# All 22 side blocks projected in one pass per token part, and TensorE's and VectorE's order fixed in both scans

## The chip, the cores and the metric

The kernel runs on one core of a Trainium2 chip. The metric is the device time of one execution in microseconds (us). The kernel before took 2149.41 us, the median of 3 runs (2149.09 to 2152.09).

## What is computed

One layer over 2048 latent tokens and 256 context tokens of 1024 channels: normalise and modulate, one wide projection, three groups of mixers (centred pooling, a bidirectional RWKV-7 scan, a bidirectional HGRN2 scan), each with a SiLU gate, then one output projection with a residual and a norm. The context only gives the scans their first state.

```python
p_lat = (_layer_norm(h_x) * (1.0 + sc_l[:, None]) + sh_l[:, None]) @ w_in[l]
p_ctx = (_layer_norm(h_ctx) * (1.0 + sc_c) + sh_c) @ w_in[l]
pv_l, u_l, fh_l, g_l = _split_proj(p_lat)
...
y_rc, y_rl = _rwkv_branch(u_c, u_l, ...)
o_hc, o_hl = _hgrn_branch(fh_c, fh_l, ...)
pool_l = _pool_branch(pv_l, True, pool_w[l], pool_scale[l])
mix_l = jnp.concatenate([pool_l, y_rl, o_hl], axis=-1) * jax.nn.silu(g_l)
new_x = _layer_norm(ALPHA * h_x + gt_l[:, None] * (mix_l @ w_out[l])) * ln_g[l] + ln_b[l]

# one step of the RWKV scan (per head, per token)
S = (S * w_t[:, :, None, :] - sa[..., None] * (kk_t * a_t)[:, :, None, :]
     + v_t[..., None] * k_t[:, :, None, :])
# one chunk of the HGRN scan
o = inter + jnp.einsum('bhts,bhsv->bhtv', scores, i_c)
S = (jnp.exp(g_last[:, :, 0, :])[..., None] * S
     + jnp.einsum('bhsk,bhsv->bhkv', k_c * jnp.exp(g_last - g), i_c))
```

## The kernel before

The program has four stages, one after the other.

**Front** (to about 508 us). It normalises x, keeps the normalised x in DRAM (`s_x`), projects the channels that RWKV needs, and forms RWKV's chunk operands.

**RWKV scan.** 36 chunks of 64 tokens (4 of context, 32 latent) are scanned in both directions at once, one `step` (L847) per chunk. On TensorE (PE) a step has `py` (state times kr), mask products into the same tile, `pu`, and `zp` (L883; its tile is also named `pu`). VectorE (DVE) adds the old state (`tz`, L887) and multiplies by the decay (`zbd`, L889), which the next step's `py` reads. ScalarE copies `pp` and `uv` in between. Work ahead of a step: `start` (L703) loads a chunk's operands, forms the products `pa` and masks them on DVE into `at`; `gather` (L754) writes 32x32 blocks to DRAM (`sd`); every 4 chunks `solve` (L768) loads 96 such systems as `m` and solves them by substitution in 31 pairs of DVE instructions (L779 a product into `tm`, L782 a subtraction from `o`), and writes `so`; `merge` (L806) loads from `so` (tile `nn`), transposes it on DVE, and completes the inverse with small PE products. `solve` runs LEAD (7) chunks ahead of the step that needs it. The loop at L942 has one iteration per chunk, and calls pieces of these generators (`go`) in an order written by hand. Inside `manual_schedule` that order is PE's; the other engines' order is chosen by the scheduler, which takes instructions as it thinks them ready.

**The filler** (L529). Beside the scan, PE projects the 22 blocks of 128 channels that RWKV doesn't need (HGRN's q, z of both directions and i; pooling; the gates). The unit between two yields is 6 of the 24 matmuls of a block on up to 512 tokens: three groups of 8 (high by high, low by high, high by low half of a split fp32). `split` makes the halves of x: a cast on ScalarE (`fxh`) and a difference on DVE (`fxl`). GpSimd splits the weights (`fwl`). `Beside` (L635) paces it: each call adds a number to what is due and runs whole units; after a BORDER, where a token part begins, it holds for HOLD calls. 18 blocks over three token parts run in the RWKV scan (R_FIL: from iteration -6, 9.4 units in each, the rest at the scan's end). Two pool blocks and two gate blocks follow in HGRN over three parts of their own, for which x is loaded and split once more.

**HGRN scan.** A window of 256 context or latent tokens (9 windows, each direction) has `hlevels` (L1004): loads, ScalarE activations, the diagonal scores (`pd`, L1055: 6 matmuls of 128x128 by 2 columns, then one DVE product into `sc`, L1056), and levels in which PE forms scores, DVE copies them under a mask (L1046), multiplies `qp` (L1069) and `tot` (L1072), GpSimd `ks`. `hsteps` (L1077) transposes `ks` into `kt`, and walks the window's 4 chunks: PE's `po` and `ps`, DVE's state `sbd` (L1116). `out_weights` (L1121) loads w_out in eight slices through one buffer `fwf`, scales each by the gate on GpSimd (L1128), casts on ScalarE (`fxh`, `woh`; L219), and takes the difference on DVE (`fxl`, `wol`; L220). The pieces of all these are given due times (`at`, L652), sorted and emitted (`follow`, L657); the scheduler then sets each engine's order.

**Output.** Pooling, readouts, gates, the output projection and the last norm, from about 1911 us on.

## Time and profile before

| | |
|---|---|
| median of 3 runs | 2149.41 us (2149.09 to 2152.09) |
| the profiled execution's own time | 2153.85 us |
| its span | 2151.8 us |
| mean granted clock of TensorE | 0.903 |
| PE busy | 1877.4 us (87%), 18306 instructions |
| PE weight load busy | 1593.8 us (74%) |
| DVE busy | 1470.2 us (68%), 3045 |
| ScalarE (ACT) busy | 954.1 us (44%), 1809 |
| GpSimd (POOL) busy | 808.4 us (38%), 729 |

The span runs from the first to the last record of the profiled execution; its own time is 2.05 us longer. The shares are means over four stages that differ, so they don't say what bounds any one of them. Weight load overlaps PE's matmuls. The clock is what the throttle granted TensorE, as a share of full speed.

### The profile page before, as it was taken

To read this page: it belongs to the slowest core of one execution; us is meant where nothing else is said; L and a number is where in the kernel's file an instruction comes from. 1 tells how busy PE (TensorE), PEld (TensorE's weight loads), DVE (VectorE), ACT (ScalarE), POOL (GpSimd) and SP (SyncE) were. 2 spreads that over 40 slices of the span, in tenths; PEclk is the share of its full clock that TensorE was granted. 3 is DMA by queue.
4 is the path that set the end of the run, shared out by engine and by line. 5 is a ranking of instruction groups with operands and counts; after the bars stand their busy time and mean duration, and the time that the engine had idled before them with its cause. 6 is when DMAs were issued, how large, how long until landed. Compare 5 with 4: busy or idle time off the path is not lost. (4 is left out here: it accounts for less than half of the span.)

```text
span 2151.8 us, 46723 instructions
## 1 busy us (share of the span) xinstructions
PE 1877.4 (87%) x18306; PEld 1593.8 (74%) x18306; DVE 1470.2 (68%) x3045; ACT 954.1 (44%) x1809; POOL 808.4 (38%) x729
## 2 busy tenths in 40 slices
PE   4788899994989979999979999968989998878996
PEld 1677788893777768877868788757877776657896
DVE  2788899886546646475473762189788788879862
ACT  3876786663123333333333233455444645322321
POOL 0144355545211322322323323454334435624653
PEclk7899999996999989999979999968888997589998
DMA  6544444328655565655666444442322323545531
GB/s 247 195 136 144 142 131 126 106 74 252 187 147 150 171 184 164 182 143 164 174 180 192 139 129 136 152 132 82 109 81 70 124 80 115 176 150 187 194 128 59
DMA packets 290915, 313.68 MB, mean 146 GB/s; under 512 B 85572, under 2 KB 246468, under 8 KB 289672
## 3 DMA queue, kind: packets, MB, share of 16 engines
q1 hardware_dynamic: 280680, 280.29, 43.3%
q10 hardware_dynamic: 4896, 17.83, 2.5%
q0 software_dynamic: 5120, 12.59, 1.8%
q8 instruction: 144, 2.36, 0.5%
q14 instruction: 75, 0.61, 0.1%
HBM read 213.88 MB, written 96.74 MB: 144 GB/s over the span
## 5 line engine op out<-in xcount | busy, mean ns | idle before, releaser
L220 POOL TENSOR_TENSOR fwl<-fwf,fwh 128x1024 fp32r<-128x1024 f32 x66 | 158.7, 2405 | 422.3 <-ACT fwh L219 369.3
L565 PE MATMUL fps<-fxh,fwh 128*128 128x512 f32 (+1 forms) x952 | 230.7, 375 | 31.0 <-ACT fxh L219 28.4
L565 PE MATMUL fps<-fxl,fwh 128*128 128x512 f32 (+1 forms) x952 | 217.2, 362 | 0.0
L565 PE MATMUL fps<-fxh,fwl 128*128 128x512 f32 (+1 forms) x952 | 211.6, 357 | 0.0
L565 PEld LDWEIGHTS fps<-fxh,fwh 128*128 128x128 f32 x952 | 160.4, 201 | 63.4 <-ACT fxh L219 34.7
L565 PEld LDWEIGHTS fps<-fxl,fwh 128*128 128x128 f32 x952 | 160.2, 199 | 24.1 <-issue 1.0
L565 PEld LDWEIGHTS fps<-fxh,fwl 128*128 128x128 f32 x952 | 158.7, 196 | 23.8
L779 DVE TENSOR_TENSOR tm<-m,o 96x31 f32<-96x31 f32 (+15 forms) x279 | 117.4, 421 | 60.3 <-DMA m<-sd 52.2
L904 POOL TENSOR_TENSOR ys<-ys,pp 64x384 f32<-64x384 f32 x64 | 76.6, 1196 | 198.7 <-ACT ys L901 191.6
L336 PE MATMUL ps<-xh,wh 128*128 128x258 f32 x768 | 125.4, 304 | 17.5 <-ACT wh L219 11.9
L1116 DVE SCALAR_TENSOR_TENSOR sbd<-sbd,tot,ps 64x64 f32<-64x64 f32 x432 | 120.5, 279 | 25.7 <-PE ps L1111 16.7
L1044 PE MATMUL pl<-qb,ks 128*64 128x64 f32 x2304 | 108.4, 252 | 30.3 <-DVE sc L1046 22.9
L1039 ACT COPY qb<-qp 64x384 f32<-64x384 f32 x192 | 99.6, 519 | 77.7 <-DVE qp L1069 33.8
L724 DVE TENSOR_TENSOR at<-pa,cst 128x384 f32<-128x384 f32 x144 | 74.1, 548 | 81.9 <-PE pa L722 81.8
L336 PEld LDWEIGHTS ps<-xh,wh 128*128 128x128 f32 x768 | 106.0, 198 | 30.6 <-ACT wh L219 13.3
L1044 PEld LDWEIGHTS pl<-qb,ks 128*64 128x64 f32 x2304 | 94.1, 161 | 45.5 <-issue 29.3
L782 DVE TENSOR_TENSOR o<-o,tm 96x31 f32<-96x31 f32 (+15 forms) x279 | 115.8, 415 | 8.3
L336 PE MATMUL ps<-xh,wl 128*128 128x258 f32 x768 | 118.6, 294 | 0.0
L1069 POOL TENSOR_TENSOR ks<-ks,tot 128x384 f32<-128x384 f32 x90 | 90.5, 1014 | 74.6 <-PE pl L1044 72.7
L336 PE MATMUL ps<-xl,wh 128*128 128x258 f32 x768 | 116.0, 289 | 0.0
L336 PEld LDWEIGHTS ps<-xh,wl 128*128 128x128 f32 x768 | 104.6, 196 | 5.7 <-issue 5.2
L336 PEld LDWEIGHTS ps<-xl,wh 128*128 128x128 f32 x768 | 102.3, 192 | 4.9 <-issue 4.6
(230 smaller groups left out, 4449.0 us busy)
## 6 DMA issues: line engine op xcount, KB each, us to landing
fwf<-in_w_in_dram SPq DMA_DIRECT2D x66, 512.0 KB, 4.2
xt<-in_x_dram ACTq DMA_DIRECT2D x32, 512.0 KB, 4.9
s_kr<-kr SPq DMA_DIRECT2D x54, 256.0 KB, 2.3
s_bk<-bk SPq DMA_DIRECT2D x54, 256.0 KB, 2.5
bks<-s_bk SPq DMA_DIRECT2D x72, 192.0 KB, 3.2
krs<-s_kr SPq DMA_DIRECT2D x72, 192.0 KB, 3.5
bk<-s_bk SPq DMA_DIRECT2D x72, 192.0 KB, 3.0
kr<-s_kr SPq DMA_DIRECT2D x72, 192.0 KB, 3.1
```

The source lines that it names most:

```text
L220: eng.tensor_tensor(out=wl, in0=wf, in1=wh.bitcast(F32), op=ALU.subtract)
L336: PE.matmul(ps[:, 0:TG + 2], a[:, k, :], b[:, k, :], start=(i == 0), stop=(i == 23))
L565: PE.matmul(ps[:, 0:n], a[:, k, :], b[k][:, o:o + n], start=(i == 0), stop=(i == 23))
L724: V.tensor_tensor(out=at[:, h], in0=pa[h], in1=cst[:, C_MASK[d]].unsqueeze(1).broadcast_to([P, NPR, P]), op=ALU.mult)
L779: V.tensor_tensor(out=tv, in0=m[:, j:j + 1, j + 1:32].broadcast_to([nrow, na, nb]), in1=o[:, 0:na, j:j + 1].broadcast_to([nrow, na, nb]), ...
L782: V.tensor_tensor(out=o[:, 0:na, j + 1:32], in0=o[:, 0:na, j + 1:32], in1=tv, op=ALU.subtract)
L904: G.tensor_tensor(out=ys[vr], in0=ys[vr], in1=pp[d][vr], op=ALU.add)
L1039: S.copy(out=qb[hh, :, :, h, :].rearrange("q p c (i b) -> q (p c) i b", b=b), in_=src[hh].rearrange("q p (c i j b) -> q (p c) i j b", c=nc ...
L1044: PE.matmul(pl[64 * (c % 2):64 * (c % 2) + 64, :, p, c // 2, :], ks[:, p, CH * c:CH * c + CH], qb[:, p, c, :, :], start=True, stop=True)
L1069: eng.tensor_tensor(out=v_, in0=v_, in1=tv[:, :, :, 1 - par:2 - par].broadcast_to([P, NPR, nb, b]), op=ALU.mult)
L1116: V.scalar_tensor_tensor(out=sn[hh, p, hh], in0=so_[hh, p, hh], scalar=tot[hh, p, c:c + 1], in1=ps[hh, p, :], op0=ALU.mult, op1=ALU.add)
```

## The change

**The filler** takes all 22 blocks in each of the three token parts (context and tokens 0 to 511; 1280 to 2047; 512 to 1279), so x is loaded and split once. The loads of x are issued two slices ahead, across parts too. The split of a part's 8 slices is spread over four BORDER yields, two slices each; HOLD is gone, and a call to the pacer ends at a BORDER. 20 units run ahead of the RWKV loop and 7.6 in each of its 43 iterations; what is left goes to HGRN, 2.2, 1.9 or 1.0 units a slot.

**Order.** `manual_schedule` now covers PE and DVE, in the RWKV loop and in HGRN: DVE's instructions, too, stand in program order. In the RWKV loop `solve` has a yield behind its load of `m`, and the load is issued at the end of the iteration that gathers its last chunk; `merge` issues its loads one yield ahead of the transposes. In HGRN the due times are replaced by 14 slots per window: each runs one piece of a level (`l0`, `l1`) and of the steps of the window before (`s0`, `s1`, `k0`, `k1`), and some filler. In the iteration before the last the rest of the filler runs in the first slot and a slice of w_out after each slot.

**The diagonal** changes its form: per direction and window it takes 12 matmuls instead of 6, each of 64 rows of q by 64 columns of `hsl`, with 128 columns moving, and two DVE products of half the size. **`kt`** is copied by ScalarE in two pieces, not three.

```diff
-R_FIL = (-6, 9.4)
+R_FIL = (20, 7.6)
+H_FIL = (2.2, 1.9, 1.0)
...
     def filler(parts, blocks):
-        for part in parts:
+        def load(part, k):
+            xs = fp.tile([P, FTOK], F32, name="fxs", bufs=2)
+            o = 0
+            for t0, n in part:
+                QX.dma_start(out=xs[:, o:o + n], in_=s_x[:, k, t0:t0 + n])
+                o += n
+            return xs
+        xs = [load(parts[0], k) for k in range(2)]
+        for pi, part in enumerate(parts):
...
-                split(xs[:, 0:n_all], xh[k][:, 0:n_all], xl[k][:, 0:n_all], V)
+                split(xs[k % 2][:, 0:n_all], xh[k][:, 0:n_all], xl[k][:, 0:n_all], V)
+                if k + 2 < KB:
+                    xs[k % 2] = load(part, k + 2)
+                elif pi + 1 < len(parts):
+                    xs[k % 2] = load(parts[pi + 1], k % 2)
+                if k % 2:
+                    yield BORDER
...
             G.memset(o.rearrange("q a t -> q (a t)")[:, 0:32 * 32:33], -1.0)
+            yield 1
             for j in range(31):
...
                 ws[n][d]["uv"] = uv
+            yield 1
             ab = [(sub(0, 0), sub(0, 1)), (sub(1, 1), sub(1, 0))]
...
-        with tc.manual_schedule(engines={mybir.EngineType.PE}):
+        with tc.manual_schedule(engines={mybir.EngineType.PE, mybir.EngineType.DVE}):
+            for _ in range(KB // 2):
+                pace(0)
+                next(fill)
+            run(fill, R_FIL[0])
             for n in range(-LEAD, NCH):
...
                 go("late", n + 1, late)
+                go("mer", n + 1, merge)
                 solving(7)
...
                 go("stp", n, step, None)
+                if s_ % SB == SB - 1:
+                    go("sol", s_ // SB, solve)
                 beside(n, 0.22)
             for k, g in gen.items():
                 run(g)
-            run(fill1)
...
-                pd = psl.tile([P, 2, NPR, nm], F32, name="pl")
-                for m in range(nm):
+                pd = [psl.tile([P, NPR, nm, CH], F32, name="pl") for _ in range(2)]
+                for h in range(2):
+                    hh = slice(64 * h, 64 * h + 64)
                     for p in range(NPR):
-                        PE.matmul(pd[:, :, p, m], q[:, p, P * m:P * m + P], hsl[:, 3 * d + p, :], start=True, stop=True)
...
+                        qc = q[hh, p].rearrange("q (m c t) -> q m c t", c=2, t=CH)
+                        for c in range(2):
+                            PE.matmul(pd[h][64 * c:64 * c + 64, p], hsl[hh, 3 * d + p, :], qc[:, :, c, :],
+                                      start=True, stop=True)
+                    V.tensor_tensor(out=sc[:, h].rearrange("q p m t -> q (p m) t"),
+                                    in0=cst[:, C_DIAG].unsqueeze(1).broadcast_to([P, NPR * nm, CH]),
+                                    in1=pd[h].rearrange("q p m t -> q (p m) t"), op=ALU.mult)
...
-        for n in range(1 + T // HWIN):
+        slots = ("k0 l0", "k0 l1", "k1 l0", "k1 l1", "s0 l0", "s0 l1", "s1 l0", "s1 l1", "s0 l0", "s0 l1", "s1 l0",
+                 "s1 l1", "l0", "l1")
+        prep = {6: 1, 11: 1}
...
+        with tc.manual_schedule(engines={mybir.EngineType.PE, mybir.EngineType.DVE}):
...
+            for n in range(nw + 1):
+                for si, slot in enumerate(slots):
+                    for what in slot.split():
+                        d = int(what[1])
+                        if what[0] == "l" and n < nw:
+                            run(lev[d, n], 1)
+                        elif what[0] != "l" and n > 0:
+                            run(stp_[d, n - 1], 1)
...
+                    if n < nw - 1:
+                        pace(H_FIL[0] if n == 0 else H_FIL[1] if n < 3 else H_FIL[2])
+                    elif n == nw - 1:
+                        run(fill if si == 0 else ow, None if si == 0 else 1)
...
+            run(ow)
```

How it moves DVE's instructions shows at two places. In the changed program the same source lines have other numbers: L779 and L782 of `solve` are L778 and L781, L724 is L722, L220 is L214, L1046 is L1050, L1069 is L1077, L1072 is L1080.

The first is a solving iteration of the RWKV scan, on DVE, from `solve` to the step's `tz` and `zbd`. A solve's instruction on `tm` shows by its size how far the substitution has come: 96x31 is the first of 31, 96x231 the eleventh, 96x255 the fifteenth. Before:

```order
L779 TENSOR_TENSOR tm<-m,o 96x252
L782 TENSOR_TENSOR o<-o,tm 96x14x18
L779 TENSOR_TENSOR tm<-m,o 96x255
L887 TENSOR_TENSOR tz_11812<-pu,zbd_5987 128x384
L887 TENSOR_TENSOR tz_11815<-pu,zbd_5989 128x384
L782 TENSOR_TENSOR o<-o,tm 96x15x17
L889 TENSOR_TENSOR zbd_5986<-tz_11812,dms_5994 128x384
L889 TENSOR_TENSOR zbd_5988<-tz_11815,dms_5995 128x384
```

And in the changed program:

```order
L781 TENSOR_TENSOR o<-o,tm 96x10x22
L778 TENSOR_TENSOR tm<-m,o 96x231
L887 TENSOR_TENSOR tz_9615<-pu,zbd_5987 128x384
L889 TENSOR_TENSOR zbd_5986<-tz_9615,dms_5994 128x384
L887 TENSOR_TENSOR tz_9618<-pu,zbd_5989 128x384
L889 TENSOR_TENSOR zbd_5988<-tz_9618,dms_5995 128x384
L823 STREAM_TRANSPOSE nn<-nn 32x192
L826 STREAM_TRANSPOSE at_7728<-nn 32x6x32 x2
L722 TENSOR_TENSOR at_9303<-pa,cst 128x384 x2
L761 STREAM_TRANSPOSE tr<-at_9303 32x192 x2
L781 TENSOR_TENSOR o<-o,tm 96x11x21
```

Where 29 instructions of a solve stood ahead of `tz` in this iteration, 21 do now; the transposes of `nn` and `at` of the next chunk follow `zbd`, and only then the solve goes on.

The second is DVE in the last window of HGRN that has levels, at the slices of w_out (`fxl` and `wol`, whose sources are the casts `fxh` and `woh` of the loaded slice `fwf`). Before:

```order
L1069 TENSOR_TENSOR qp_21111<-qp_21111,tot_21243 128x192x2
L220 TENSOR_TENSOR fxl_21953<-fwf,fxh_21952 128x768
L220 TENSOR_TENSOR wol_21957<-fwf,woh_21956 128x256
L1056 TENSOR_TENSOR sc_21116<-cst,pl 128x768
L1046 COPY_PREDICATED sc_21098<-cst,pl 128x384
L1069 TENSOR_TENSOR qp_21093<-qp_21093,tot_21288 128x96x4
L220 TENSOR_TENSOR fxl_21964<-fwf,fxh_21963 128x768
L220 TENSOR_TENSOR wol_21968<-fwf,woh_21967 128x256
L1046 COPY_PREDICATED sc_21116<-cst,pl 128x384
```

And in the changed program:

```order
L1065 TENSOR_TENSOR sc_21085<-cst,pl 128x384 x2
L214 TENSOR_TENSOR fxl_21175<-fwf,fxh_21174 128x768
L214 TENSOR_TENSOR wol_21179<-fwf,woh_21178 128x256
L1050 COPY_PREDICATED sc_21079<-cst,pl 128x384
L1077 TENSOR_TENSOR qp_21074<-qp_21074,f_20829 128x384
L1080 TENSOR_TENSOR tot_21207<-f_20829 128x384
L214 TENSOR_TENSOR fxl_21213<-fwf,fxh_21212 128x768
L214 TENSOR_TENSOR wol_21217<-fwf,woh_21216 128x256
L1050 COPY_PREDICATED sc_21085<-cst,pl 128x384
L1077 TENSOR_TENSOR qp_21080<-qp_21080,f_20841 128x384
L1080 TENSOR_TENSOR tot_21242<-f_20841 128x384
```

The slices, which the scheduler had put where it took them to be ready, stand at fixed places now, one level's work (`sc`, `qp`, `tot` of one direction) apart.

## Rows read from the trace of the kernel before

**Rows 1.** Stretches of 100 us: busy us and instructions by engine, TensorE clock, DMA.

```profile
core 0: us, PE busy (x) PEld busy (x) DVE busy (x) ACT busy (x) POOL busy (x), PEclk, DMA share, GB/s
1200.00:1300.00 100.00, 97.59 (x1219) 83.46 (x1219) 61.63 (x142) 36.03 (x79) 31.20 (x26) 1.00 0.50 140
1400.00:1500.00 100.00, 76.99 (x718) 61.26 (x717) 93.01 (x178) 54.71 (x95) 49.14 (x39) 0.74 0.34 104
```

**Rows 2.** Timeline, TensorE: starts of state steps (start us, us, engine, line, tiles).

```profile
618.94 1.50 PE L858 MATMUL py<-zbd,kr 128*128 128x128 f32 x12
...
636.57 1.50 PE L858 MATMUL py<-zbd,kr 128*128 128x128 f32 x12
...
682.22 1.50 PE L858 MATMUL py<-zbd,kr 128*128 128x128 f32 x12
...
1064.36 1.50 PE L858 MATMUL py<-zbd,kr 128*128 128x128 f32 x12
...
1082.73 1.50 PE L858 MATMUL py<-zbd,kr 128*128 128x128 f32 x12
...
1121.28 1.50 PE L858 MATMUL py<-zbd,kr 128*128 128x128 f32 x12
...
1375.09 1.50 PE L858 MATMUL py<-zbd,kr 128*128 128x128 f32 x12
```

**Rows 3.** Timeline of one solving step: TensorE's `zp`, then DVE to `tz`.

```profile
1006.19 0.92 PE L883 MATMUL pu<-uv,bt 128*64 128x64 f32 x24
...
1012.85 0.42 DVE L782 TENSOR_TENSOR o<-o,tm 96x252 f32<-96x252 f32 x1
...
1013.64 1.01 DVE L887 TENSOR_TENSOR tz<-pu,zbd 128x384 f32<-128x384 f32 x2
```

**Rows 4.** The same, 1398 to 1911: all; L565 (filler); tile po; fcs; fxs.

```profile
1398.00:1911.00 513.00, 449.65 (x5120) 366.30 (x5120) 433.45 (x938) 255.14 (x459) 221.68 (x186) 0.82 0.33 103
...
1398.00:1911.00 513.00, 119.37 (x480) 83.86 (x480) 0.82 0.33 103
...
1398.00:1911.00 513.00, 130.64 (x1152) 102.47 (x1152) 0.00 (x0) 15.33 (x32) 0.82 0.33 103
...
1398.00:1911.00 513.00, 41.30 (x84) 0.82 0.33 103
...
1398.00:1911.00 513.00, 29.02 (x24) 17.92 (x24) 0.82 0.33 103
```

**Rows 5.** Timeline, TensorE: filler matmuls of 512 and of 256 columns.

```profile
534.64 1.98 PE L565 MATMUL fps<-fxl,fwh 128*128 128x512 f32 x8
536.45 1.98 PE L565 MATMUL fps<-fxh,fwh 128*128 128x512 f32 x8
...
549.52 1.12 PE L565 MATMUL fps<-fxh,fwh 128*128 128x256 f32 x8
550.47 1.12 PE L565 MATMUL fps<-fxh,fwl 128*128 128x256 f32 x8
```

**Rows 6.** Waits of DVE in 619 to 1385: total us, times, longest.

```profile
DVE nn L823 <- DMA nn<-so: 84.1, 22, 6.7
...
DVE tm L779 <- DMA m<-sd: 45.8, 8, 7.6
```

**Rows 7.** Timeline, DVE: first diagonal product of window 1 and of the last.

```profile
1424.49 0.95 DVE L1056 TENSOR_TENSOR sc<-cst,pl 128x768 f32<-128x768 f32 x1
...
1838.58 0.94 DVE L1056 TENSOR_TENSOR sc<-cst,pl 128x768 f32<-128x768 f32 x1
```

**Rows 8.** Timeline: two slices of w_out, one after the other.

```profile
1840.60 0.96 DVE L220 TENSOR_TENSOR fxl<-fwf,fxh 128x768 fp32r<-128x768 f32 x1 [0.30 <-ACT fxh L219]
...
1848.86 1.05 DVE L220 TENSOR_TENSOR fxl<-fwf,fxh 128x768 fp32r<-128x768 f32 x1 [3.91 <-ACT fxh L219]
```

**Rows 9.** Timeline, TensorE: 12 products of half the rows, 12 diagonal products.

```profile
541.98 0.94 PE L722 MATMUL pa<-krs,bks 64*128 64x128 f32 x12
...
1475.72 2.72 PE L1055 MATMUL pl<-hsl,q 128*128 128x2 f32 x12
```

83 lines of the change are left out of this document (36 added, 47 removed).

## The prediction

> **What bounds the kernel now.** I read the table of stretches first, then the starts of the state steps, then the waits of VectorE (DVE), then the stretch of the second scan. The reader should see four things.
>
> The RWKV scan is bound by TensorE (PE) where nothing disturbs it: 97.6% busy at a granted clock of 1.00 in a stretch in its middle [rows 1]. Its 36 state steps start between 618.94 and 1375.09, so 35 intervals take 756 us [rows 2]. An undisturbed step takes 18.4 us (1064.36 to 1082.73). Two kinds stand out: steps beside a triangular solve, 45.7 us for a pair (636.57 to 682.22), and two steps in which the filler changes its token part, of which one runs from 1082.73 to 1121.28, 38.6 us [rows 2].
>
> In a solving step DVE's row of work is the bound: TensorE begins `zp` (a `pu` tile in the trace, L883) at 1006.19, and DVE comes to `tz`, which reads it, at 1013.64, behind solve instructions [rows 3].
>
> The HGRN scan has DVE busy 433 of 513 us and PE 450, at a clock of 0.82: neither is full, and both are late to each other [rows 4]. In its first 100 us PE is 77% busy and the clock 0.74, with DVE at 93% [rows 1]: PE waits there while x is split a second time.
>
> **The sum, part by part.** One unit is what the filler does between two yields, 6 matmuls. Eight matmuls of 512 columns start 1.81 us apart from the next eight, eight of 256 columns 0.95 us [rows 5]: 1.36 and 0.71 us a unit, so 1.04 in a part of 512+256 columns and 1.10 over all parts. There are 119 groups of 24 matmuls, 476 units, before and after. Before, 396 of them belong to the RWKV scan (9.4 per iteration) and 80 to HGRN. Now 20 run ahead of the loop and 7.6 per iteration for 43 iterations; less the 8 borders that make 346 calls into 338 units; 138 are left to HGRN.
>
> *Up to step 0.* Before, the six iterations with filler ahead of step 0 ran 56 units; now 20 + 7 x 7.6 = 73. 17 more at 1.10: **+19 us**.
>
> *Steps 0 to 35.* Some 20 intervals are light ones: 1.8 units less at 1.04, -1.9 us each, -38. I assume that the chain py, pp, pu, uv, zp, tz, zbd, which fitted into a light step of 18.4 us, fits into 16.5 too. The 13 solving intervals are not PE's: a full solve is 62 DVE instructions, most of which fall into two iterations, and they must still be done. But 21 of them now stand ahead of `tz` in the first of the two, where before the scheduler put up to 29: 8 instructions of 0.42 us [rows 3] are 3.4 us a pair, in 7 pairs: between 0 and -24, and since all of them must still run before the next `tz` but one, I take -7. The two part changes: x comes in through two buffers, of which both loads are now started a part ahead, and the split is spread over four border yields, so I take 26 us instead of 38.6 for each: -26 (bounds 0, if the later loads still stall PE, and -40, two plain steps). Then costs: 4 of the 10 pooling segments now lie in this loop, on DVE's fixed row, and the wait for `m` too: +8. Together **-63 us**.
>
> The wait for `m` deserves a weighing. DVE waits 45.8 us in 8 times for the load of `m`, and 84 us in 22 times for `nn` [rows 6]. The `nn` loads now go out one yield, about half an iteration, before DVE needs them. The load of `m` now goes out at the end of the iteration that gathers its last chunk, so DVE meets it as the first thing of the next one, with `at`, `tz` and `zbd` queued behind it. In a step `tz` is not needed until PE has done py, the mask products, pu and a filler piece, some 9 us, and the 21 solve instructions ahead of it take some 7: most of a 5.7 us wait is in that slack or is worked off behind `zbd`. The nearest rows give 0 to 46 us, I put 4 of the +8 on it. The Trainium skill, "TensorE: Matmul & The Clock Gate", section "Architectural detail: the array is 16× 32×32, not 1× 128×128", says that ScalarE's and VectorE's queues are strictly first in, first out. By that rule taken at its hardest, all 45.8 us stand in the chain and the sum is 42 us worse; the row of before can't decide it, since there the scheduler had put the wait where little was behind it.
>
> *Into HGRN.* Before, from the last step's start to the first diagonal product of window 1 it is 1375.09 to 1424.49, 49 us [rows 2, 7], with a tail of filler and then eight splits of x that PE waits for. Now: 7 us of the last step, then iteration 0, 14 slots x 2.2 units x 1.04 = 32 us that fill PE while the context's levels run on DVE and GpSimd, and 7 for the ramp: 46. **-3 us**.
>
> *The windows.* Before, diagonals come at 1424.49 first and 1838.58 for the last window, so 59 us a window, and the stage ends at 1911: 487 us [rows 7]. PE's scan work per window: 450 less the filler's 119 and some 20 for context and pooling, over 8: 39 us at this clock; of that 131/8 = 16 are products into `po` [rows 4]. DVE's: 433 less 41 (pooling scans and differences) and 29 (second split of x, gone), over 8.5: 43 [rows 4]. So iteration 1 (context steps give no output): 39 - 16 + 26.6 units x 1.04 = 51; iteration 2: 67; iterations 3 to 6: 39 + 14 x 1.04 = 53 each, PE's, with DVE's 43 beneath; iteration 7, without filler, DVE's 43; the steps alone at the end 20. Iteration 8 is worse than it was. The eight slices of w_out go through one buffer: load, GpSimd product, ScalarE casts, DVE split, and the next load waits for that split. The splits of two slices that followed each other stand at 1840.60 and 1848.86, 8.3 us [rows 8]; I take 8.8, since a load can queue. In the new order they stand after slots 1 to 8, one level apart on DVE, so DVE and with it the scan wait there: 7 x 8.8 = 62, and 20 for the other slots, 82 where 43 would do. Sum 51 + 67 + 212 + 43 + 82 + 20 = 475: **-12 us**.
>
> *The diagonal.* The 12 matmuls of a window (both directions) with 2 columns take 2.72 us; now 24 on half the rows with 128 columns. Twelve such take 0.94 [rows 9], so 24 take 1.9: 8 windows x -0.8, -6 at best; at the old pace each, +22. Nearest to the 0.94, but PE is not the bound everywhere: 0. The merged copies of `kt` save 18 ScalarE copies on an engine that is half idle: 0, and nothing is lost if that cover goes.
>
> Sum: 19 - 63 - 3 - 12 = -59. From the profiled execution's 2153.85 us (span 2151.8) that is 2095; the median of the runs shown, 2149.41, lies 4.4 below that execution, so **2090 us**. The front stage and the output stage I leave as they are.
>
> **Rivals.** (a) *Both scans run at their engines' sums.* DVE's waits shrink in the solving pairs to 42 us (-24 instead of -7), w_out's slices cost 8.3 each and hide part (-10), and the upper clock holds in HGRN, where filler is in every slot: 39 at 0.82 is 34 at 0.95, of which I count 3, since DVE's 43 lie close beneath, in 5 windows: -15. 2090 - 42 = **2048**. For it: the clock of 1.00 where PE is never starved [rows 1]. [...]
>
> (b) *DVE's row in the RWKV scan is held by its loads.* All of `m`'s wait is in the chain, +42: **2132**, and with stalled splits of x (+26) 2158. The skill's first-in, first-out sentence would bear this out.
>
> (c) *The slots of HGRN go in lockstep, slower than before.* In a slot DVE's `sbd`, mask copy, `qp`, `tot` wait for PE's products, and PE's next slot for `sbd` and `qp`. If nothing overlapped, a slot would be 39/14 = 2.8 us of PE's and 43/14 = 3.1 of DVE's, 5.9, and 14 of them 83 us a window instead of some 53. It decides from about three tenths of the slots: 0.29 x 30 x 7 windows = 61 us eats the whole gain; with half of them 2090 + 105 = **2195**. For it: DVE was free to take what was ready in the scheduler's order, and is not now. Against: consecutive slots belong to different directions, so a level has two slots' time.
>
> (d) *The order hardly differs in effect*: **2149**. Against it: 58 units change stage and 24 splits go.
>
> **How the numbers follow.** Forecast 0.54, (a) 0.17, (b) 0.10, (c) 0.15, (d) 0.04. A measurement of this kernel can tell about 0.2%, 4.3 us. Faster takes the forecast, (a) and half of (b): 0.76; same (d) and 0.02 of (b): 0.06; slower (c) and the rest of (b): 0.18. The range, 2040 to 2155, takes in the bounds of the part changes, the diagonal and `m`, (a) and most of (b), and leaves out (c). The likeliest case's own range is 2060 to 2125.
>
> **What would show it.** Step 0 starts near 638; 20 light steps of 16 to 17 us; solving pairs of 42 to 46; no step above 30; last step near 1331; windows of 53 us with PE above 95% and a clock above 0.9; then one window of some 82 us in which DVE waits for w_out's casts. I am wrong if windows 3 to 6 take over 60 us, if DVE's wait for `m` is followed by PE waiting for `zbd`, or if the window of w_out is no longer than its neighbours.

## The result, and the profile after

The changed kernel took 2276.62 us, the median of 4 runs (2247.26 to 2289.25), beside 2150.75 us for the kernel before: the ratio is 1.0495, with a 95% interval of 1.0422 to 1.0568. Two of these four runs, and one each of two experiments below (2257.65 and 2160.07 us), were over 1.5% longer than the fastest run of the same kernel and stand in the medians but not in the ratios; the changed kernel's other two took 2247.26 and 2270.32 us. It is slower, where the forecast was 2090 us and faster. The profiled execution took 2270.32 us, with a span of 2268.3.

On the page of the changed kernel (the span, the busy time of each engine, and the clock in 40 slices), PE and DVE are busy for nearly as long as before (1877.4 and 1470.2 us then). The time is in the gaps and in the clock, which has two slices of 5 tenths near the end, where it had one before:

```profile
span 2268.3 us, 46855 instructions
...
PE 1903.9 (84%) x18498; PEld 1608.1 (71%) x18498; DVE 1471.0 (65%) x3037; ACT 930.7 (41%) x1763; POOL 792.9 (35%) x729
...
PEclk7899999987998978998979889999988687559998
```

The table of stretches of the changed kernel: up to state step 0, the 35 intervals to the last step, the seven windows between the first and the last diagonal product, and from there to the last output products of HGRN.

```profile
core 0: us, PE busy (x) PEld busy (x) DVE busy (x) ACT busy (x) POOL busy (x), PEclk, DMA share, GB/s
510.00:646.61 136.61, 107.09 (x668) 87.56 (x667) 50.33 (x126) 26.88 (x42) 30.15 (x21) 0.86 0.57 167
646.61:1433.22 786.61, 662.39 (x7862) 555.59 (x7861) 463.01 (x996) 244.00 (x515) 202.01 (x183) 0.90 0.52 146
1481.96:1903.20 421.24, 380.45 (x4645) 313.49 (x4642) 305.51 (x698) 200.41 (x355) 159.41 (x139) 0.88 0.27 83
1903.20:2019.72 116.52, 82.04 (x808) 65.43 (x805) 62.16 (x149) 24.69 (x48) 38.92 (x28) 0.53 0.31 103
```

[rows 1] had a stretch in the middle of the RWKV scan with PE 97.6% busy at a clock of 1.00; over the whole scan it was 92% at 0.95 before, and is 84% at 0.90 now. The scan of the kernel before, with the columns as above:

```profile
618.94:1375.09 756.15, 696.70 (x8289) 592.44 (x8288) 415.57 (x929) 257.78 (x542) 218.83 (x184) 0.95 0.57 161
```

Cut at the events that [rows 2] and [rows 7] show, the two profiled spans divide like this (us). "Last `po`" is the first of the last six products into `po` that read `sbd`; it starts at 1909.25 before and at 2019.24 after (the last stretch above ends 0.5 us behind it).

| | to step 0 | 35 steps | to first diagonal | 7 windows | to last `po` | to the end |
|---|---|---|---|---|---|---|
| before | 618.9 | 756.2 | 49.4 | 414.1 | 70.7 | 242.6 |
| after | 646.6 | 786.6 | 48.8 | 421.2 | 116.0 | 249.0 |
| difference | +27.7 | +30.4 | -0.6 | +7.1 | +45.3 | +6.5 |

The differences add up, to 0.1 us, to the difference of the spans, 116.5. The largest surprise is the second column, which was to be -63. What happens there shows in one step, from 1122.66 to 1154.87. TensorE's rows (start us, us, engine, line, tiles, then the idle time before and who ended it):

```profile
1125.09 0.89 PE L720 MATMUL pa<-krs,bks 64*128 64x128 f32 x12
...
1134.25 2.11 PE L720 MATMUL pa<-krs,bks 64*128 64x128 f32 x12 [3.84 <-DVE at L722]
...
1143.75 2.08 PE L626 MATMUL pa<-fe,pw 128*128 128x512 f32 x2 [5.82 <-DVE at L722]
...
1154.87 1.50 PE L858 MATMUL py<-zbd,kr 128*128 128x128 f32 x12
```

And DVE's rows of the same step:

```profile
1123.54 3.94 DVE L612 TENSOR_TENSOR_SCAN fcs<-cst,fpu 128x80 f32<-128x80 f32 x8 [5.53 <-ACT fpu L610]
...
1130.34 0.18 DVE L778 TENSOR_TENSOR tm<-m,o 96x31 f32<-96x31 f32 x1
...
1133.64 1.01 DVE L722 TENSOR_TENSOR at<-pa,cst 128x384 f32<-128x384 f32 x2
...
1139.39 0.40 DVE L778 TENSOR_TENSOR tm<-m,o 96x231 f32<-96x231 f32 x1
1139.71 0.55 DVE L887 TENSOR_TENSOR tz<-pu,zbd 128x384 f32<-128x384 f32 x1
...
1143.14 1.02 DVE L722 TENSOR_TENSOR at<-pa,cst 128x384 f32<-128x384 f32 x2
```

PE makes a chunk's `pa` from 1125.09 on, and DVE should mask it into `at`. There are two `pa` buffers, and several products of PE take turns in them. On the fixed row the pooling sums (`fcs`, `fe`, 1123.54 to 1130.4) and seven solve instructions stand first, so `at` comes at 1133.64. PE's next `pa` (L720, 1134.25) needs that buffer, and waits 3.84 us. Fourteen more solve instructions then stand ahead of `tz` (1139.71), behind `tz` stand `zbd` and three transposes, and only then comes the second `at` (1143.14). PE, whose next work also needs a `pa` buffer (L626), waits 5.82 us. The step lasts 32.2 us. Over the whole scan, PE's waits for `at` in the table of waits (total us, times, longest):

```profile
PE pa L831 <- DVE at L722: 50.0, 15, 7.6
PE pa L597 <- DVE at L722: 17.9, 5, 8.1
PE pa L626 <- DVE at L722: 13.4, 3, 5.8
PE pa L720 <- DVE at L722: 12.7, 3, 5.7
```

In the kernel before, the same table has these:

```profile
PE pa L831 <- DVE at L724: 22.6, 9, 4.6
...
PE pa L595 <- DVE at L724: 6.7, 3, 4.1
...
PE pa L722 <- DVE at L724: 0.6, 2, 0.3
```

That is 94.0 us after and 29.9 before, 64.1 more. All of PE's idle time in the scan, its length less PE's busy time, rose by 64.7 us, from 59.5 to 124.2; its busy time fell by 34.3, as the filler's units left. The two make the +30.4. DVE's own waits after:

```profile
DVE at L722 <- PE pa L720: 133.0, 16, 13.9
...
DVE tm L778 <- DMA m<-sd: 47.4, 7, 8.1
```

The wait for `m` is nearly what it was (45.8 us in [rows 6]). The wait for `nn` of 84.1 us in [rows 6] is gone from the table: the earlier loads did their part. In its place DVE now waits 133.0 us for `pa` (56.6 before), and PE waits for DVE: each is late to the other.

The intervals can be sorted by what DVE executes in them. Light ones (at most 15 solve instructions) took 19.3 us on average before (20 of them) and take 18.5 now (16). Solving ones took 22.2 (12) and take 24.3 (11). Those with a new part's splits took 103 us together (3 intervals) and take 105.5 (4). The four with pooling sums, which the kernel before did not have here, take 118.8.

### The profile page after: what moved, and what is told of

The parts are those of the page before. It is cut to its first block, busy times and chain, and to the rows that moved or that the text cites. A ratio compares the mean times of both kernels' runs of the same rounds, so it can differ in the third digit from the quotient of the medians.

```text
span 2268.3 us, 46855 instructions
## 1 busy us (share of the span) xinstructions
PE 1903.9 (84%) x18498; PEld 1608.1 (71%) x18498; DVE 1471.0 (65%) x3037; ACT 930.7 (41%) x1763; POOL 792.9 (35%) x729
## 5 line engine op out<-in xcount | busy, mean ns | idle before, releaser
L214 POOL TENSOR_TENSOR fwl<-fwf,fwh 128x1024 fp32r<-128x1024 f32 x66 | 159.7, 2420 | 416.3 <-ACT fwh L213 300.1
L567 PE MATMUL fps<-fxh,fwh 128*128 128x256 f32 (+1 forms) x952 | 234.1, 380 | 23.9 <-ACT fxh L213 22.3
L567 PE MATMUL fps<-fxl,fwh 128*128 128x256 f32 (+1 forms) x952 | 230.9, 376 | 0.0
L567 PE MATMUL fps<-fxh,fwl 128*128 128x256 f32 (+1 forms) x952 | 217.2, 363 | 0.4 <-POOL fwl L214 0.4
L722 DVE TENSOR_TENSOR at<-pa,cst 128x384 f32<-128x384 f32 x144 | 73.4, 551 | 202.5 <-PE pa L720 188.0
L567 PEld LDWEIGHTS fps<-fxl,fwh 128*128 128x128 f32 x952 | 168.1, 208 | 28.2 <-issue 4.7
L778 DVE TENSOR_TENSOR tm<-m,o 96x31 f32<-96x31 f32 (+15 forms) x279 | 114.9, 412 | 63.9 <-DMA m<-sd 54.7
L904 POOL TENSOR_TENSOR ys<-ys,pp 64x384 f32<-64x384 f32 x64 | 69.7, 1088 | 226.3 <-ACT ys L901 222.9
L330 PEld LDWEIGHTS ps<-xh,wh 128*128 128x128 f32 x768 | 106.0, 198 | 29.9 <-ACT wh L213 12.7
L781 DVE TENSOR_TENSOR o<-o,tm 96x31 f32<-96x31 f32 (+15 forms) x279 | 115.7, 415 | 9.0
L1077 POOL TENSOR_TENSOR ks<-ks,tot 128x384 f32<-128x384 f32 x90 | 85.3, 952 | 102.1 <-issue 70.3
L1048 PE MATMUL pl<-qb,ks 128*64 128x64 f32 x2304 | 101.1, 246 | 14.8 <-DVE tot L1080 7.9
L1048 PEld LDWEIGHTS pl<-qb,ks 128*64 128x64 f32 x2304 | 87.2, 156 | 26.2 <-issue 17.0
```

The source lines that it names most:

```text
L214: eng.tensor_tensor(out=wl, in0=wf, in1=wh.bitcast(F32), op=ALU.subtract)
L330: PE.matmul(ps[:, 0:TG + 2], a[:, k, :], b[:, k, :], start=(i == 0), stop=(i == 23))
L567: PE.matmul(ps[:, 0:n], a[:, k, :], b[k][:, o:o + n], start=(i == 0), stop=(i == 23))
L722: V.tensor_tensor(out=at[:, h], in0=pa[h], in1=cst[:, C_MASK[d]].unsqueeze(1).broadcast_to([P, NPR, P]), op=ALU.mult)
L778: V.tensor_tensor(out=tv, in0=m[:, j:j + 1, j + 1:32].broadcast_to([nrow, na, nb]), in1=o[:, 0:na, j:j + 1].broadcast_to([nrow, na, nb]), ...
L781: V.tensor_tensor(out=o[:, 0:na, j + 1:32], in0=o[:, 0:na, j + 1:32], in1=tv, op=ALU.subtract)
```

## The experiments

Each run is the changed kernel with one edit, unless its text says more. The table gives the same stretches for all of them (profiled execution), and the median of the runs. The two runs that leave the RWKV loop as it is in the changed kernel (HGRN's DVE free, w_out spread) show how far the 35 steps move by themselves: 792.1 and 786.9, beside 786.6.

| run | to step 0 | 35 steps | to first diagonal | 7 windows | to last `po` | to the end | median us |
|---|---|---|---|---|---|---|---|
| RWKV's DVE free | 651.5 | 743.1 | 49.6 | 420.0 | 115.1 | 249.4 | 2232.39 |
| HGRN's DVE free | 648.1 | 792.1 | 57.3 | 403.3 | 73.7 | 241.2 | 2217.54 |
| no pooling sums | 651.2 | 772.5 | 49.7 | 396.0 | 120.8 | 223.3 | 2216.76 |
| w_out spread | 646.7 | 786.9 | 48.7 | 441.4 | 89.1 | 240.2 | 2249.60 |
| solve behind `tz` | 649.4 | 752.7 | 49.0 | 400.0 | 115.5 | 242.6 | 2218.53 |
| both DVE rows free | 650.7 | 739.7 | 58.6 | 403.7 | 79.5 | 244.9 | 2174.18 |
| both free, 9.4 units | 653.3 | 777.6 | 58.0 | 338.4 | 88.0 | 242.1 | 2165.01 |
| solve behind, HGRN free, 9.4 units | 662.8 | 785.3 | 56.5 | 348.0 | 86.3 | 244.0 | 2187.29 |
| both free, 9.0, nothing ahead | 622.3 | 766.5 | 50.3 | 369.3 | 87.0 | 242.7 | 2139.82 |
| wait for `m` behind | 648.5 | 772.3 | 48.6 | 405.5 | 115.2 | 241.9 | 2244.55 |
| both free, 8.3, nothing ahead | 621.8 | 750.2 | 57.4 | 401.5 | 72.5 | 246.5 | 2149.93 |

**DVE's row in the RWKV scan.** The first run frees it:

```diff
-        with tc.manual_schedule(engines={mybir.EngineType.PE, mybir.EngineType.DVE}):
+        with tc.manual_schedule(engines={mybir.EngineType.PE}):
             for _ in range(KB // 2):
```

> The changed kernel with DVE's order in the RWKV scan left to the scheduler again (TensorE's stays fixed; HGRN as changed). Theory: the 786.6 us from the first to the last state step (756.2 before, 693 forecast) are long because on DVE's fixed row the mask copies `at`, which free TensorE's `pa` buffers, and `tz` stand behind a solve's pieces and the pooling sums; freed, the 35 steps take 690 to 740 us and the whole 2195 to 2235 us. Rival: the filler's new shape (pooling inside this scan, other pace, other loads) is what lengthens the steps, whoever orders DVE; then the steps stay at 775 to 800 and the whole at 2260 to 2290.

Measured: 2232.39 us (2214.11 to 2240.88), ratio to before 1.0346 (1.0283 to 1.0408); the steps take 743.1 us, which is 43.5 less. PE's waits for `at` in this run:

```profile
PE pa L831 <- DVE at L722: 26.7, 11, 5.4
PE pa L720 <- DVE at L722: 10.8, 10, 3.0
...
PE pa L597 <- DVE at L722: 9.2, 3, 5.0
PE pa L626 <- DVE at L722: 9.1, 3, 4.3
```

They sum to 55.8 us where 94.0 stood. The total lies inside the theory's range, the steps just above it. But the rival has a share too: with DVE free the steps are only 13 us shorter than before, not 63, so half of what was missed here (43.5 of 93.4 us are the order's) is not the order. The `at` waits fell by 38 us and PE's idle time in the scan by 34, to 89.8; the other 9 us are its busy time, at a granted clock of 0.92 instead of 0.90.

**DVE's row in HGRN.** The same edit at the second `manual_schedule`.

> The changed kernel with DVE's order in HGRN left to the scheduler again (RWKV as changed). Theory: only the window of the w_out slices is hurt by DVE's fixed row (116.5 us from the last diagonal to the last output product, 74.0 before), the seven windows before it are TensorE's; freed, the last part takes 70 to 85 us, the seven windows stay near 421, the whole 2230 to 2245 us. Rival: all slots go in lockstep on the fixed row; then the seven windows, too, fall from 421 to 360 to 390 and the whole to 2160 to 2200 us.

Measured: 2217.54 us (2217.34 to 2227.49), ratio 1.0304 (1.0250 to 1.0357). The last part is 73.7 us, 3 more than before the change: the fixed row costs 42.3 us there. The total lies between the two expectations, because the windows fell to 403.3 as well. Of these 17.9 us, 11 are PE's idle time, which fell from 40.8 to 29.7 us; PE's waits for DVE's `sc` ahead of the diagonal products (L1063), 19.9 us in 12 times in the changed kernel, are 0.8 here. The other 7 are busy time, and these need not be DVE's doing. The run with the solve moved has HGRN exactly as the changed kernel, and its seven windows took 400.0 us. Its row of stretches, then that of the run with HGRN's DVE free (columns as above):

```profile
1451.10:1851.10 400.00, 360.44 (x4644) 297.05 (x4640) 305.05 (x698) 200.41 (x355) 160.18 (x139) 0.94 0.28 87
```

```profile
1497.40:1900.70 403.30, 373.56 (x4650) 310.05 (x4648) 305.28 (x715) 207.53 (x367) 174.10 (x146) 0.90 0.32 100
```

In both PE is over 90% busy, as it is in the changed kernel's 421.24 us. The granted clock was 0.88 in the changed kernel, 0.94 and 0.90 here. The rival of lockstep, which had the windows at 360 to 390, falls: the fixed row costs some 11 us of PE's time in them.

**The slices of w_out.** They begin one window earlier and DVE's differences stand two slots behind the load:

```diff
+                late_ = []
...
-                    split(wf[:, c], wh, wl, V)
+                    S.copy(out=wh, in_=wf[:, c])
+                    late_.append((wl, wf[:, c], wh))
                     wo[k, j] = (wh, wl)
                 yield 1
+                yield 1
+                for wl, wfc, wh in late_:
+                    V.tensor_tensor(out=wl, in0=wfc, in1=wh.bitcast(F32), op=ALU.subtract)
...
-                    if n < nw - 1:
+                    if n < nw - 2:
...
-                    elif n == nw - 1:
-                        run(fill if si == 0 else ow, None if si == 0 else 1)
+                    elif n < nw:
+                        run(fill if n == nw - 2 and si == 0 else ow, None if n == nw - 2 and si == 0 else 1)
```

> The changed kernel with the w_out slices spread: they begin one window earlier, where no filler is left, and the DVE differences of a slice stand two slots behind its load. Theory: DVE's wait for the casts (30.2 us in 7 times) and TensorE's for `sbd` behind it make the last part 116.5 us; spread, the last part takes 75 to 85 us, the window before it no more than 5 us longer, and the whole is 2235 to 2250 us. Rival: the last part is long because without filler TensorE falls to the lower clock (0.50 granted there), and the slices only fill its gaps; then the last part stays above 105 us and the whole at 2260 to 2290 us.

Measured: 2249.60 us (2224.10 to 2257.65), ratio 1.0398 (1.0317 to 1.0478). The last part fell from 116.0 to 89.1 us, and DVE's wait for the casts in it (total us, times, longest) to this:

```profile
DVE fxl L1149 <- ACT fxh L1143: 7.2, 2, 3.7
```

But the windows before it took 441.4 us instead of 421.2, all of it in the last of the seven (64.5 us where 44.6 stood). So the last part got shorter with the wait, though not to the 75 to 85 us of the theory, and the window before it became 20 us longer and not 5 at most: moving the slices gave back only some 7 us of the profiled time. The total is inside the theory's range all the same. In the changed kernel itself, one slice goes like this (loads of `fwf` land, GpSimd multiplies, ScalarE casts, DVE takes the difference, and only behind that the state `sbd`):

```profile
1921.76 2.34 POOL L1137 TENSOR_TENSOR fwf<-fwf,fwh 128x1024 f32<-128x1024 f32 x1 [4.11 <-DMA fwf<-in_w_out_dram]
1924.13 0.83 ACT L213 CAST fxh<-fwf 128x768 fp32r<-128x768 f32 x1 [3.71 <-POOL fwf L1137]
...
1924.99 0.96 DVE L214 TENSOR_TENSOR fxl<-fwf,fxh 128x768 fp32r<-128x768 f32 x1 [5.31 <-ACT fxh L213]
...
1926.20 1.83 DVE L1125 SCALAR_TENSOR_TENSOR sbd<-sbd,tot,ps 64x64 f32<-64x64 f32 x6
...
1926.84 1.94 PE L1110 MATMUL po<-sbd,qp 128*64 128x128 f32 x6 [11.46 <-DVE sbd L1125]
```

PE stands idle for 11.46 us ahead of 1926.84, since its `po` reads `sbd`, whose DVE instruction stands behind the slice. In this part of the changed kernel DVE waits for the casts:

```profile
DVE fxl L214 <- ACT fxh L213: 30.2, 7, 5.3
```

While PE starves here the granted clock is 0.53 on average (the last row of the stretches above), 0.76 in the kernel before. From 1920 to 2022 it was 0.50, the lower of its two levels, 1.2 GHz, and PE's own work is longer too: some 800 instructions are busy for 82 us here, and for 66.7 us in the run with HGRN's DVE free, where the clock was 0.71.

**The pooling sums.** This run leaves out the scan, the two differences, the count multiply and the last difference of the pooling; a ScalarE copy of the projection takes their place.

```diff
-            for r in range(nr):
-                V.tensor_tensor_scan(out=cs[:, r, :], data0=cst[:, C_PRST], data1=pu[:, r, :], initial=0.0,
-                                     op0=ALU.mult, op1=ALU.add)
...
+            S.copy(out=pd_[:, 0:n], in_=ps)
```

> The changed kernel without the pooling sums: the scan, the differences and the count multiply on DVE are left out, a ScalarE copy of the projection goes to the pooling product instead. Theory: the steps of 32 to 33 us (from 689.4, 1122.7 and 1154.9) are pooling sums and a solve on one row ahead of `at` and `tz`; without the sums they are 20 to 25 us, the RWKV steps take 745 to 765 us in all and the whole is 2230 to 2250 us. Rival: the long steps are the solve's and its load's alone; then the RWKV steps change by under 10 us and the whole by under 20.

Measured: 2216.76 us (2210.56 to 2221.92), ratio 1.0283 (1.0239 to 1.0328). The steps are 14.1 us shorter, less than the theory's 22 and more than the rival's 10. The three steps that the theory names fell from 33.4, 32.2 and 32.8 to 28.9, 26.8 and 23.8, so that one of them came into its 20 to 25. The whole fell by more than either expected, but the rest came in the windows (-25) and in the output stage (-26). The first is little more than the runs below show between kernels with HGRN in the same order, at a clock of 0.92 instead of 0.88. In the output stage DVE was busy for 140.5 us instead of 173.8: of its readouts, for one, 3 of 8 reductions into `ss` had already run beside the last part of HGRN, where the changed kernel had none. What let them start earlier was not followed.

**Where the solve stands.** DVE's order stays fixed; every piece of the solve goes behind `tz`, `zbd` and the masks:

```diff
-                solving(7)
                 go("sc", s_, start)
-                solving(7)
                 go("sc", s_ + 1, start)
                 go("stp", n, step)
                 beside(n, 0.22)
-                solving(7)
                 go("stp", n, step, 2)
...
-                solving(7)
+                solving(10)
                 beside(n, 0.34)
-                solving(7)
+                solving(11)
...
-                solving(7)
+                solving(11)
```

> The changed kernel, DVE's order still fixed in both scans, with every piece of the solve moved behind the step's `tz` and `zbd` and the two mask copies, in three lots of 10, 11 and 11 an iteration. Theory: not that the order is fixed costs, but that 14 solve instructions and the wait for `m` stand ahead of `at` and `tz`; behind them, TensorE's waits for `at` fall from 94 us to under 50, the 35 steps take 735 to 755 us (786.6), the whole 2225 to 2245. Rival: any fixed row costs, since the solve's 13 us an iteration hold the next transposes and masks wherever it stands; then the steps stay at 775 or more and the whole within 12 us of 2276.

Measured: 2218.53 us (2211.26 to 2227.97), ratio 1.0321 (1.0283 to 1.0358); the steps take 752.7 us, 33.9 less. PE's largest waits for `at`:

```profile
PE pa L831 <- DVE at L722: 28.7, 12, 8.7
PE pa L720 <- DVE at L722: 26.9, 9, 7.8
...
PE pa L597 <- DVE at L722: 11.5, 5, 3.1
```

They are 67.1 us (70.4 with one smaller row), above the 50 that I expected, but the steps came out in the theory's range, and the whole 6 us below it. So most of the cost is not that the row is fixed, but where the solve stands in it: a better place gives 34 of the 43.5 us that a free row gave.

**The wait for `m` alone.** Only the three lots ahead of `tz` in the first of a solve's two iterations are left out, and the solve ends 20 instructions later in the second:

```diff
-                def solving(k):
+                def solving(k, ahead=False):
...
-                            go("sol", g, solve, k)
+                            first = n == SB * g + SB - LEAD
+                            go("sol", g, solve, 0 if ahead and first else 7)
...
-                solving(7)
+                solving(7, True)
```

> The changed kernel with DVE's order fixed in both scans; only in the first of the two iterations of a solve its three lots ahead of `tz` are left out, so that the wait for the load of `m` and the solve's first pieces stand behind `tz`; the second iteration keeps its 20 ahead of `tz`, and 20 follow. Theory: the wait for `m` (47.4 us in 7 times on the changed kernel's DVE) is most of what the fixed row costs in this scan; the 35 steps take 745 to 760 us (786.6), like the 752.7 with every lot behind. Rival: the lots themselves ahead of the masks are the cost, in both iterations alike; then half of that gain, 765 to 775 us.

Measured: 2244.55 us (2234.18 to 2261.55), ratio 1.0417 (1.0367 to 1.0467); the steps take 772.3 us, 14.3 less. DVE has no wait for `m` left in this run, and PE's waits for `at` are still these:

```profile
PE pa L831 <- DVE at L722: 50.7, 13, 11.2
PE pa L597 <- DVE at L722: 19.1, 5, 10.5
PE pa L626 <- DVE at L722: 14.9, 3, 6.8
...
PE pa L720 <- DVE at L722: 8.9, 4, 4.9
```

Their sum is 93.6 us, as in the changed kernel. The row of the scan (columns as above):

```profile
648.53:1420.85 772.32, 649.39 (x7862) 543.11 (x7861) 464.06 (x996) 244.18 (x515) 203.14 (x183) 0.91 0.52 148
```

By the number the rival is right: the wait for `m` with the lots of that iteration is some 14 us, not most of the cost. But PE's idle time did not fall, 122.9 us instead of 124.2: the 14 us are the busy time of as many instructions, 649.4 instead of 662.4, at a clock of 0.91 instead of 0.90. With the wait for `m` gone from DVE, PE waits for DVE as long as before; why the clock was higher is not shown.

**Both rows free.** The two edits of the first two runs together.

> The changed kernel with DVE's order left to the scheduler in both scans (TensorE's fixed in both). Theory: the two freed parts add: steps 743 us, the last part 75, windows 403, together some 2165 to 2180 us, so that nearly all of the loss is DVE's fixed row and what is left is the 28 us by which the first step starts later. Rival: the gains overlap, since a faster RWKV scan hands HGRN its work at the lower clock; then 2190 to 2215.

Measured: 2174.18 us (2167.75 to 2179.00), ratio 1.0102 (1.0076 to 1.0128). The gains add, as the theory said: by the profiled spans the two runs alone gave 39.6 and 52.8 us, and both edits together 91.2 of the 116.5 that the change cost. By the runs that the ratios count it is 85 of 108. What is left, 25 us of span, is less than the 31.8 by which step 0 starts later than before, at 650.7.

**The filler's pace.** Both rows free, and, against the changed kernel,

```diff
-R_FIL = (20, 7.6)
+R_FIL = (20, 9.4)
-H_FIL = (2.2, 1.9, 1.0)
+H_FIL = (1.5, 0.5, 0.4)
```

> As the one with DVE free in both scans, and the filler's pace in the RWKV scan back at 9.4 units an iteration (HGRN gets what is left, 1.5, 0.5 and 0.4 a slot). Theory: with 7.6 units TensorE idles some 90 us in the RWKV scan, because the steps' chains and not its work set their length, so lighter steps gave nothing; 69 more units cost 20 to 40 us there and save some 60 in HGRN: 20 to 40 us faster than with both free alone, at 2130 to 2155. Rival: the steps are TensorE's, each unit costs its 1.04 us in either scan: no difference over 10 us.

Measured: 2165.01 us (2155.09 to 2185.10, 10 runs), ratio 1.0075 (1.0038 to 1.0112): 9 us faster than the run before by the medians, so that the theory's range was missed and on the total the rival is right. The profiled stretches say more. 378 more matmuls of the filler in the RWKV scan, 63 units, went with 37.9 us more there, 0.60 us each; 414 fewer in the seven windows, 69 units, with 65.3 less, 0.95 each. A unit is cheaper in the RWKV scan, where PE has gaps (90.8 us idle without these units, 70.9 with them), but not free.

The same pace with DVE fixed in the RWKV scan and the solve behind `tz`, HGRN free:

> DVE's order fixed in the RWKV scan with the solve behind `tz`, free in HGRN, and 9.4 units an iteration. Theory: a fixed row with the solve behind the chain is as good as the scheduler's: the steps take within 15 us of those of the run with DVE free in both scans and the same pace, the whole 2125 to 2160. Rival: the pooling sums, which still stand ahead of `at` on the fixed row, and the transposes behind the solve make the steps 25 us or more longer than there: 2160 to 2190.

Measured: 2187.29 us (2172.16 to 2199.04), ratio 1.0169 (1.0118 to 1.0220). The steps take 785.3 us, 7.7 longer than with the free row, within the 15 of the theory; the whole is 9.6 us later at step 0 and 9.6 slower in the windows, and so inside the rival's range. For the steps the theory held, for the total the forecast did not.

**The units ahead of step 0.** Both rows free, and the splits and units in front of the RWKV loop go (shown against the run with 9.4 units):

```diff
-R_FIL = (20, 9.4)
+R_FIL = (0, 9.0)
-H_FIL = (1.5, 0.5, 0.4)
+H_FIL = (1.6, 1.0, 0.7)
...
-            for _ in range(KB // 2):
-                pace(0)
-                next(fill)
-            run(fill, R_FIL[0])
```

> DVE free in both scans, the first part's splits and the 20 units ahead of the RWKV loop left to the loop's own pace (9.0 units an iteration, HGRN 1.6, 1.0 and 0.7 a slot). Theory: step 0 starts at 647 to 653 in every run with units ahead (618.94 before), because x's first splits and 20 units stand on TensorE ahead of the chain mask, solve, merge that leads to step 0; without them it starts at 618 to 630, the later steps do not give it all back, and the whole is 2130 to 2150 us. Rival: the units only move; the scan is longer by what step 0 is earlier, and the whole stays at 2155 to 2180.

> DVE free in both scans, no splits and no units ahead of the RWKV loop, 8.3 units an iteration (so that about as many are left to HGRN as in the changed kernel), HGRN's pace as changed. Theory: against the run with both free and 20 units ahead (step 0 at 650.7, 2174 us) step 0 comes 20 to 30 us earlier and the 35 steps take 5 to 12 us more: 2150 to 2165 us. Rival: no gain, 2168 to 2185.

The second of the two has `R_FIL = (0, 8.3)` and HGRN's pace as changed. Measured: with 9.0 units, 2139.82 us (2125.89 to 2160.07, 11 runs), ratio to before 0.9915 (0.9884 to 0.9947). With 8.3 units, 2149.93 us (2139.92 to 2165.63, 10 runs), ratio 0.9973 (0.9945 to 1.0001), and so not told apart from before. Step 0 starts at 622.3 and 621.8, and beside the run with both rows free (650.7) and about the same pace in HGRN, the steps give back 10.5 of the 28.9 us. For step 0 the theory held in both; the totals lie inside its range with 9.0 units and at its edge with 8.3. The scan and the windows of the faster one (columns as above):

```profile
622.28:1388.73 766.45, 694.73 (x8161) 584.65 (x8160) 455.42 (x993) 256.65 (x537) 217.20 (x190) 0.95 0.55 156
1439.10:1808.30 369.20, 332.05 (x4442) 273.69 (x4439) 286.60 (x699) 195.28 (x340) 149.15 (x135) 0.91 0.27 84
```

This is the only run whose interval lies below the kernel before, though by less than 2%: it keeps the 22 blocks per part, the single split of x and the slots of HGRN, and lets the scheduler order DVE.

## Why the prediction was wrong

*Up to step 0 (+19 forecast, +27.7 measured).* I priced 17 more units and left out what the splits of x do in front of them. From 508 us to step 0, 438 matmuls of the filler ran instead of 330: 18 units more, for 91.6 us of PE's busy time instead of 68.7. PE's idle time there rose by 9 us, to 30.9, and its other work fell by 4. Two rows of the changed kernel, TensorE:

```profile
530.67 0.80 PE L567 MATMUL fps<-fxh,fwh 128*128 128x512 f32 x1 [5.59 <-ACT fxh L213]
...
623.89 2.11 PE L720 MATMUL pa<-krs,bks 64*128 64x128 f32 x12 [10.54 <-DVE at L722]
```

PE waits for casts of x at 530.67, one of four such waits of 16 us in all, and 10.54 us for `at` at 623.89. Without splits and units ahead step 0 comes 28 us earlier than in the run with both rows free (622.3 beside 650.7).

*Steps 0 to 35 (-63 forecast, +30.4 measured).* This step failed most. The filler left, as forecast: PE's busy time fell by 34 us. What failed is the overlap: the sum put nothing on PE's waits for `at`, and they rose from 29.9 to 94.0 us. By its terms:
- "21 of them now stand ahead of `tz` in the first of the two, where before the scheduler put up to 29" was read from one pair. Counted over all `tz` of the two programs, solve instructions ahead of `tz` are 16 to 31 in the first interval of a pair before and 21 now, and 31 to 46 in the second and 41 now. On average that is 4 fewer in the first and 5 more in the second: there was nothing to gain. And I followed only `tz`: PE in fact waits for `at`, which frees its `pa` buffers and which on the fixed row stands behind lots of the solve and the pooling sums. The run with RWKV's row free gives 43.5 us back, the one with the solve moved 33.9.
- The wait for `m`: I put 4 us on it between 0 and 46, and the run without it gave 14.3, together with the 21 solve instructions that were taken along, and 1.3 of it in PE's idle time. So rival (b), that all of this wait is in the chain, is not what happened. The Trainium skill's sentence on first-in, first-out queues ("TensorE: Matmul & The Clock Gate", section "Architectural detail: the array is 16× 32×32, not 1× 128×128") agrees with the trace, where `at`, whose `pa` was done at 1125.98, starts at 1133.64, behind the sums and the seven solve instructions that stand ahead of it. But the price that I set beside it was for the wrong wait: it is less the load that holds the row than the pieces themselves.
- The light steps gave 0.8 us each, not 1.9 in 20: that the chain "fits into 16.5 too" held for the best of them (16.1 at the least), but only 16 stayed light, and the four with pooling took 118.8 us. I had put +8 on pooling and `m` together.
- The part changes were to give 26 us. They moved over four intervals instead of three, 105.5 us in all. Beyond as many light steps that is 31 us instead of 45: some 14 us gained.

*Into HGRN (-3 forecast, -0.6 measured)* was right in that the filler fills PE there (46.5 of 48.7 us busy, at a clock of 1.00). That the sum came out is in part luck: the filler takes 40.5 us of it, put at 32, and the rest less than the 14 I gave it.

*The windows (-12 forecast for all; +7.1 and +45.3 measured).* The slices of w_out were right in mechanism and price: on DVE the eight stand from 1907.48 to 1968.11, 8.7 us apart, where I took 8.8. The last part was to take 82 + 20 = 102 us and took 116.0, because the 51 us behind the last slice were put at 40; the low clock there is in no term of the sum. The run with HGRN's DVE free takes 42.3 of the 45.3 us back.

The seven windows before it were to take 51 + 67 + 212 + 43 = 373 us and took 421.2. One step that failed here is the filler's price, "26.6 units x 1.04". The row of the filler's tile `fps` in the changed kernel, first in the RWKV scan, then in the seven windows, and last in the windows of the run with the solve moved (columns PE, PE's weight load and ScalarE, then clock, DMA share, GB/s):

```profile
646.61:1433.22 786.61, 355.18 (x1549) 268.19 (x1548) 32.30 (x64) 0.90 0.52 146
1481.96:1903.20 421.24, 146.08 (x648) 105.79 (x648) 13.12 (x28) 0.88 0.27 83
1451.10:1851.10 400.00, 140.10 (x648) 101.23 (x648) 13.10 (x28) 0.94 0.28 87
```

648 matmuls are 108 units, so a unit is busy for 146.08/108 = 1.35 us in these windows, and for 1.30 in the third row. [rows 4] had said so beforehand: 119.37 us for 480 matmuls, 1.49 a unit. My sum took the filler out of the 450 us at that price and put it back at 1.04, which is a distance of starts in an undisturbed stretch ([rows 5]) and not a busy time. That is not a matter of the stage: by the first row a unit is busy for 355.18/258 = 1.38 us in the RWKV scan too. 108 x 0.31 = 33 us of the missing 48 is that.

The run with the solve moved has HGRN in the same order and took 400.0 us: 27 over the forecast, and its price of 1.30 accounts for 28. The 21 us by which the changed kernel's windows are longer still lie in windows 4 and 5 (67.5 and 72.5 us, 58.1 and 58.7 in the other run). The two windows together in the changed kernel, then in the run with the solve moved (columns as in the stretches):

```profile
1664.86:1804.94 140.08, 127.06 (x1339) 104.38 (x1339) 79.30 (x190) 58.67 (x100) 43.74 (x40) 0.75 0.24 72
1634.42:1751.17 116.75, 104.47 (x1339) 85.62 (x1339) 79.43 (x190) 58.61 (x100) 43.71 (x40) 0.93 0.28 86
```

PE executes as many instructions and is idle as long (13.0 and 12.3 us); its busy time is 22.6 us longer, at a clock of 0.75 instead of 0.93. What let the clock fall there is not shown. With PE at 90% busy in the windows, and 18 us less with DVE free, rival (c), lockstep, which counted from 61 us up, is not what happened, though its sign was right.

*The diagonal (0 forecast).* Its matmuls take 31.3 us in the whole kernel, where they took 35.9: for PE's work the forecast of nothing, with -6 as its best, was right, though I misread [rows 9], whose 12 diagonal products are one direction's (192 in the kernel before, 24 a window) and not both. What the sum left out is the wait of 19.9 us for `sc` that now stands ahead of these products, and is nearly gone with DVE free; before, PE waited for `sc` at the levels' products instead, 16.5 us.

*The output stage*, which I left alone, is 6.5 us longer. PE waits 15.9 us for the casts `mh` there, 10.7 before; the rest was not followed.

Of the signs of "what would show it", step 0 near 638, light steps of 16 to 17, no step above 30 and windows of 53 us throughout did not come true; two of windows 3 to 6 took over 60 us, a sign of being wrong. The longer window of w_out came as forecast, and PE's table of waits in the scan has none for `zbd`. Without DVE's fixed rows and the units ahead, and with 9.0 units an iteration, the change is worth 16 us (2139.82 beside 2155.88 for the kernel before in the same session), not 59: the rest of the gain that was forecast showed in no run.

## What to carry to other kernels

A fixed order on an engine that is only 60% busy (DVE in the RWKV scan: 463 of 787 us) is not free: what counts is not its load but what stands ahead of the one instruction that frees a buffer for the bound engine. Work with slack (a solve, pooling sums, weight splits) belongs behind that instruction, or under a scheduler that may let it pass. And background work that moves must be taken out of one stage and put into the other by the same measure: in the kernel before a unit was busy for 1.24 us in the RWKV scan, at a clock of 0.95, and for 1.44 in the seven windows, at 0.85, and neither is the 1.04 between its starts when nothing disturbs it.

## What was not expected of the hardware

The same instructions of HGRN, in the same fixed order, took 421.2, 420.0, 405.5 and 400.0 us for seven windows in four kernels that differ only before them; the granted clock was 0.88, 0.89, 0.92 and 0.94. PE was about as full in all (90 to 91%). Most of the largest difference is the two windows shown above: the same work, PE idle as long, and 22.6 us more of busy time at the lower clock. So the clock moved this stage by 5%, as much as most edits here, without any change in its order, and one profiled execution does not carry a claim on the windows. Whether what ran before them set the clock, or it falls so by chance, these runs do not tell.
